# The sums of the attention's probabilities: DMAs that accumulate in SBUF in place of additions on GpSimd

## The chip, the core and the metric

The kernel runs on one core of a Trainium2 chip. The metric is the device time of one execution in microseconds (us). The core has five engines with a queue each: TensorE (PE, matrix products), VectorE (DVE), ScalarE (ACT), GpSimd (POOL) and SyncE (SP), which here issues nearly all DMAs. The engines work on SBUF and meet through semaphores; each serves its queue in order.

## The reference, cut to what matters

One layer of a diffusion backbone over 1024 latent tokens and 128 prompt tokens: a gated feed-forward half-step, a mixer of two attention branches, and a second half-step. The mixer is where the change lies.

```python
# branch A: windowed, 8 heads; a latent token sees 256 cached keys, its own block of 128 and both neighbours, and a sink
p = jax.nn.softmax(jnp.concatenate([s_band, s_ctx, col], axis=-1), axis=-1)
o = einsum(p[..., :lb], vband) + einsum(p[..., lb:lb + lc], vc)
...
# branch B: latent, 8 heads; a latent token sees 256 cached keys and all 1024 latent keys
p = jax.nn.softmax(s, axis=-1)
return jnp.einsum('bkgqs,bskd->bqkgd', p, vf)
```

A softmax needs, for each query, the sum of the exponentials over all its keys. How the kernel adds them up is what the change touches.

## The kernel before, in words

The first feed-forward step and the projections come before the attention, the merge and the second feed-forward step after it; the attention runs from about 1148 to 1830 us. In the attention the keys lie on the partitions and the queries along the free dimension. Heads are worked one after the other: eight windowed ones (to about 1393 us), then eight latent ones.

`attend` (line 1220) works a head in units. A unit is two or three pieces of scores, each of one tile of 128 keys and up to 512 queries, put side by side in a tile of up to 1024 columns. The 1024 queries are cut into two halves of 512. A half has three units in a windowed head and five in a latent head. For each unit:

- TensorE writes the scores to PSUM (`S`, lines 1405 to 1420).
- ScalarE takes the exponential (line 1286). The first unit of a half writes it to a new tile `acc`, the others to a tile `pf`. There are two buffers of each.
- The exponentials are split into a high part `ph` (line 1290 on ScalarE, or line 1288 on VectorE in every second unit) and a low part `pl` (line 1291, a VectorE subtraction of two SBUF operands). Both parts go into the products with the values (lines 1240 and 1241), one unit later.
- In all units of a half but the first, `pf` is added to `acc` (line 1298). In a latent head that is one instruction of 128x1024 for each unit, four a half. In a windowed head a unit needs two, as its pieces cover different queries: 256 and 2x256 columns, which do not overlap, then twice 384 columns, which do. These are four a half too, 128 in the kernel.

When a half is done, `den` (line 1249) folds `acc` (line 1251: its right 512 columns are added to the left on GpSimd), and four steps of the stream later TensorE multiplies it with a column of ones (line 1256), which gives the sums over the partitions; VectorE takes the reciprocal (line 1263), and a DMA puts it into `rec_sp`, for the normalisation of the outputs (line 1456).

The order of the work is that of emission: `attend` is the main stream, and side streams advance with it at set rates (operands and maxima of the next head, the prompt's own attention, gate products and the windowed outputs' product as filling for TensorE). The attention and its side streams are placed 20 instructions ahead of what was emitted before them. Waits between engines follow from which columns of which tile an instruction reads and writes.

Of the kernel before, what the change touches and what calls it, by code (L numbers as in the profile page):

```python
# [20 lines left out]
KD = 8            # feature tiles of the model width  # L21
NL = 1024         # latent tokens
NP = 128          # prompt tokens
T = NL + NP
NB = 3            # token blocks
BW = 384
LB = 256          # latent columns of the last block
NF = 22           # feature tiles of the ffn width
NCTX = 256
NK = NCTX + NL    # keys a latent token reads  # L30
# [6 lines left out]
ADA = ((0, 4), (4, 2), (6, 4), (10, 4), (14, 4))      # first chunk of 512 modulation columns, chunks  # L37
MODS = ((0, 0), (0, 1), (1, 0), (2, 0), (2, 1), (3, 0), (3, 1), (4, 0), (4, 1))   # group and place of each

# cut of the hidden tiles, for both half-step ffns  # L40
SOLO = ((3, 3), (3, 3))   # hidden tiles that the first block runs ahead by
MID = ((2,) * 8, (2,) * 8)
END = ((2, 2, 2), (2, 2, 2))
NA = (6, 6)       # tiles of hidden activations
LAST = ((), (2,))         # blocks whose squares the tensor engine sums tile by tile
NS = 2            # tiles that those sums lag by
TT = ("t0h", "t0l", "t1h", "t1l", "t2h", "t2l")

# steps of side streams per step of the main one
NR = 3            # statistics of the first norm  # L50
NQ = 1.5          # first norm
TR = 1.4          # norm of the second ffn
AR = (2, 0.4)     # modulations, up to the first gate and after it
N2 = (0.5, 1, 2)          # norm of the mixer, by block
FR = (0.3, 1.2, 1.5)      # final norm, by block
CH = 2.6          # latent projections
PREP = (1.3, 1.3, 2.5)    # operands and maxima of the next head: windowed, latent, first latent
PROMPT = 0.5      # prompt's own attention
GRATE = (0.5, 0.7, 0.4, 0.5)   # filling work, by four heads
PR = 0.2          # normalised outputs, windowed  # L60
LR = 0.6          # normalised outputs, latent

# orders and distances
RW = 3            # steps between a block's statistics and their use
DY = 4            # steps before a denominator's product
HM = 2            # one high part in so many is cut off by the vector engine
HP, HQ = 20, 20   # instructions that attention and its side streams come ahead of
GK = 2            # feature tiles of a gate product at a time
G0 = 9            # gate steps before the first head
WN = 5            # step of the merge that loads the first output weights  # L70
# [6 lines left out]
class Build:  # L77
# [45 lines left out]
    def ahead(self, gen, n):  # L123
        """a stream whose instructions come before others emitted up to n earlier"""
        while True:
            if n:
                with self.tc.high_priority(n):
                    try:
                        next(gen)
                    except StopIteration:  # L130
                        return
            else:
                try:
                    next(gen)
                except StopIteration:
                    return
            yield
# [104 lines left out]
    def ada(self, g):  # L242
        """modulations of group g: chunks of 512 columns, each in its own rows of one bank"""
        nc, a = self.nc, self.a
        c0, n = ADA[g]
        ps = self.ps("m")

        def load(k):
            raw = self.ap.tile([P, 2048], F32, name="adaw")[:, :n * 512]
            nc.sync.dma_start(raw, a["ada_w"][k * P:(k + 1) * P, c0 * 512:(c0 + n) * 512])  # L250
            return raw
        raw = load(0)
        for k in range(KD):
            yield
            for cg in range(n):
                nc.tensor.matmul(ps[32 * cg:32 * cg + 32, :], self.cs[:, k, :],
                                 raw[:, cg * 512:(cg + 1) * 512], start=(k == 0), stop=(k == KD - 1))
            if k < KD - 1:
                yield
                raw = load(k + 1)  # L260
        yield
        r = 32 * n
        pt = self.ps("m")
        for q in range(0, 4, 2):
            ev = self.tmp(2 * P)
            nc.vector.tensor_copy(ev[:r, :], ps[:r, q * P:(q + 2) * P])
            for i in range(2):
                nc.tensor.transpose(pt[:, (q + i) * P:(q + i) * P + r], ev[:r, i * P:(i + 1) * P], self.ident[:r, :r])
        yield
        for cg in range(n):  # L270
            j = 4 * (c0 + cg)
            nc.vector.tensor_tensor(
                self.mods[g][:, cg * 4:cg * 4 + 4, :],
                pt.rearrange("p (q r) -> p q r", q=4)[:, :, cg * 32:cg * 32 + 2],
                self.adab[:, j:j + 4][:, :, None].broadcast_to([P, 4, 2]),
                op=ALU.add)
        # scale of norm i = modulation 3i+1, gate = 3i+2
        for i in range(3):
            if MODS[3 * i + 1][0] == g:
                t = self.G[i]  # L280
                nc.vector.tensor_scalar_add(t, self.mod(3 * i + 1), 1.0)
                nc.vector.tensor_mul(t, t, self.gains[:, i, :][:, :, None].broadcast_to([P, KD, 2]))
            if MODS[3 * i + 2][0] == g:
                nc.vector.tensor_scalar_mul(self.gate[i], self.mod(3 * i + 2), 0.5)
        yield

# [33 lines left out]
    def sums(self, ps, sq, start, stop):  # L320
        """sum over the features of one tile, by token on the partitions"""
# [7 lines left out]
    def stat(self, b, k):  # L329
        """sum of squares of a block, one feature tile more"""  # L330
# [78 lines left out]
    # x += gate * psum  # L409
# [51 lines left out]
    def inv(self, b, stats=False):  # L461
        """1 / rms of a block"""
        if stats:
            yield from self.stats(b)
        self.r[b] = yield from self.rstd(self.acc[b], D, RW)

    def norm_pair(self, i):
        """norm of the last two blocks, and sums of their feature halves, for seven products in place of eight;
        the sum of the first halves takes the place of the last block's own"""
# [49 lines left out]
    def gu_pair(self, wgu, j, rest, end=False):  # L519
        """gate and up of the last two blocks in seven products of halves; rest: the first block too"""  # L520
# [75 lines left out]
    def ffn(self, wgu, wd, gate, after, n, begin=None):  # L596
        """the first block runs ahead until the halves of the others are combined; they catch up at the end"""
# [68 lines left out]
    def first(self):  # L666
        """first hidden tiles of the first block, begun with the half of the features that is ready first"""
# [68 lines left out]
    def ada0(self, hf):  # L736
        """shift and scale of the first norm, for half of the features"""
# [72 lines left out]
    def mix(self):  # L810
# [52 lines left out]
        def put(dh, dl, src, w, rows=slice(0, P), shape=None):  # L863
            """two exact parts of src, to DRAM"""
# [20 lines left out]
        def keys(lh, ll, k0, n, prompt):  # L885
            """keys and values of the latent branch from columns of ckv; k0: where they go"""
# [69 lines left out]
        def ctx():  # L956
            """cached keys and values of both branches"""
# [109 lines left out]
    def chain(self, gen, rate):  # L1067
        """like spawn, but one after the other"""
# [11 lines left out]
    def gates(self):  # L1080
        nc = self.nc

        def one(i, b, w):
# [7 lines left out]
            # sigmoid(x) = (1 + tanh(x / 2)) / 2; the half goes with the residual gate  # L1091
# [40 lines left out]
    def rows(self, m, dsts):  # L1132
        # -m of [128, 8 tiles] as rows of the moving operand, in two parts
# [86 lines left out]
    def attend(self, units, S, V, scale, hid):  # L1220
        """units: two parts (key tile, q0, q1) of one width; S(ps, part) writes scores less the maximum."""
# [46 lines left out]
        for n, u in enumerate(units):  # L1268
# [23 lines left out]
            if u[0][0] != 0:  # L1292
                av = acc[hf].rearrange("p (a b) -> p a b", a=2)
                i = 0
                while i < np_:
                    a0 = u[i][1] - 512 * hf
                    m = 2 if i + 1 < np_ and u[i + 1][1] == u[i][1] else 1
                    nc.gpsimd.tensor_add(av[:, :m, a0:a0 + w], av[:, :m, a0:a0 + w], pf[:, i:i + m, :])  # L1298
# [18 lines left out]
    def prompt(self, hid):  # L1317
        """a head over the prompt's own keys"""
# [122 lines left out]
    def normed_o(self, b, br, p):  # L1441
        """outputs of two heads for a block, over their denominators, in two parts"""
# [27 lines left out]
    def fill(self):  # L1470
        """work that the attention's gaps take: gates, then the product of the windowed heads' outputs"""
# [26 lines left out]
    def merge(self):  # L1498
# [15 lines left out]
        def gated(b):  # L1514
            """sum of the gated branches"""
# [74 lines left out]
def _tables():  # L1590
# [19 lines left out]
    # key on partitions; column c stands for query - key block start = c - 256  # L1610
# [5 lines left out]
def _layout(i):  # L1616
# [3 lines left out]
    def kt(w):                    # (K, N) -> [128, K/128, N]  # L1620
        return w.reshape(w.shape[0] // P, P, w.shape[1]).transpose(1, 0, 2)

    def tiles(w):                 # (K, N) -> [N/128, 128, K]
# [10 lines left out]
    def col(v):                   # (n,) -> [128, n/128]  # L1634
# [24 lines left out]
    def small(w):                 # (256, n, 128) -> [128, n * 2 * 128]  # L1659
# [28 lines left out]
```

## Time and profile before

| | us |
|---|---|
| time, median of 3 runs | 2835.97 |
| lowest, highest | 2833.17, 2837.92 |
| span of the profiled execution (its whole time is not listed apart) | 2830.5 |
| PE busy | 2684.0 |
| DVE busy | 1910.4 |
| ACT busy | 971.5 |
| POOL busy | 776.6 |

The profile is of one execution. A span runs from the first to the last instruction; what the device spends around it is the difference to a run's time. Shares of busy time are over the whole span, and the stages differ: the attention has to be read by itself. A row of a group gives the line, engine, operation, tiles written and read, the count, the busy time and mean duration of one, and behind the bar the idle time of the engine just before them with what ended it. Matmuls overlap, so their mean duration is longer than their distance. A DMA counts as busy only for the engines that move data; the row of the issuing queue shows the issue alone.

### The profile page before, as it was taken

What the parts mean: (1) busy time and instruction counts of PE and PEld (TensorE: products, weight loads), DVE (VectorE), ACT (ScalarE), POOL (GpSimd) and SP (SyncE); (2) the same over time, 40 slices, a digit from 0 to 9 for tenths busy, and PEclk for the clock granted to TensorE, in tenths of its full rate; (3) what the DMA queues carried; (4) which work ended last, traced back from release to release, by engine and by line L of the source; (5) the groups of instructions that cost most, each with busy time, mean ns of one, the idle gap of its engine ahead of it and who ended that gap; (6) DMA issues with size and microseconds to landing.
All of it is one profiled execution on the core that took longest, in us unless ns stands there. A gap on an engine that the chain in (4) does not pass through costs nothing.

```text
span 2830.5 us, 38964 instructions
## 1 busy us (share of the span) xinstructions
PE 2684.0 (95%) x15049; PEld 2504.4 (88%) x15049; DVE 1910.4 (67%) x2979; ACT 971.5 (34%) x1492; POOL 776.6 (27%) x523
## 2 busy tenths in 40 slices
PE   7899999999999998999999888899999999999998
PEld 5699999999999897788777766689999999999998
DVE  3765555555687665777788888756685555555777
ACT  4532222222345442344334333324542222222334
POOL 2421111111323011344445444323331111111232
PEclk9899999999999998999999999999999999999999
DMA  7543332111214556223223224485421111111113
GB/s 262 171 139 97 107 112 75 45 45 46 96 52 152 180 178 186 75 80 96 80 73 99 72 77 116 148 277 189 135 89 45 46 45 45 45 46 45 60 60 112
DMA packets 159919, 290.31 MB, mean 103 GB/s; under 512 B 18158, under 2 KB 112866, under 8 KB 156406
## 3 DMA queue, kind: packets, MB, share of 16 engines
q1 hardware_dynamic: 158006, 283.10, 31.9%
q10 hardware_dynamic: 1728, 4.72, 0.4%
q8 instruction: 119, 1.95, 0.3%
q14 instruction: 66, 0.54, 0.1%
HBM read 233.71 MB, written 53.92 MB: 102 GB/s over the span
## 4 chain that ended last, share of the span: by engine, by line
PE 45%; DVE 10%; issue 2%; DMA 2%; ACT 2%; POOL 1%; SPq 0%; DVEq 0%; ACTq 0%; POOLq 0%
PE ps_g L206 7%; PE ps_g L204 7%; PE ps_g L205 7%; PE pp_m L204 4%; PE pp_m L205 4%; PE pp_m L206 4%; DVE pl L1291 3%; PE pp_o L204 1%; PE pp_o L206 1%; PE pp_o L205 1%; PE pp_o L1241 1%; DVE ph L1288 1%; PE pp_m L1212 1%; PE pp_o L1240 1%; PE ps_S L1419 1%
## 5 line engine op out<-in xcount | busy, mean ns | idle before, releaser
L204 PE MATMUL ps_g<-hh,whi 128*128 128x384 f32 x1284 | 435.3, 340 | 10.1 <-ACT hh L175 4.8
L206 PE MATMUL ps_g<-hh,wlo 128*128 128x384 f32 x1284 | 434.9, 339 | 6.0 <-DVE wlo L176 6.0
L205 PE MATMUL ps_g<-hl,whi 128*128 128x384 f32 x1284 | 435.1, 339 | 2.2 <-DVE hl L176 2.2
L543 POOL TENSOR_TENSOR adaw<-adaw 128x512 f32<-128x512 f32 x132 | 182.0, 1379 | 812.7 <-DVE wlo L176 783.6
L176 DVE TENSOR_TENSOR wlo<-raw,whi 128x1024 fp32r<-128x1024 f32 (+1 forms) x203 | 260.5, 1283 | 159.5 <-ACT whi L175 157.6
L1298 POOL TENSOR_TENSOR acc<-acc,pf 128x1024 f32<-128x1024 f32 (+3 forms) x128 | 251.6, 1971 | 406.3 <-ACT pf L1286 213.9
L175 ACT CAST whi<-raw 128x1024 fp32r<-128x1024 f32 (+1 forms) x203 | 209.5, 1033 | 410.8 <-PE ps_g L205 212.9
L175 ACT CAST whi<-adaw 128x1024 fp32r<-128x1024 f32 x132 | 138.9, 1052 | 449.4 <-PE ps_g L205 310.2
L204 PEld LDWEIGHTS ps_g<-hh,whi 128*128 128x128 f32 x1284 | 243.9, 190 | 17.9 <-ACT whi L175 6.2
L206 PEld LDWEIGHTS ps_g<-hh,wlo 128*128 128x128 f32 x1284 | 244.1, 190 | 12.3 <-DVE wlo L176 9.7
L205 PE MATMUL pp_m<-hl,whi 128*128 128x384 f32 x732 | 251.6, 344 | 0.0
L204 PE MATMUL pp_m<-hh,whi 128*128 128x384 f32 x732 | 251.3, 343 | 0.0
L205 PEld LDWEIGHTS ps_g<-hl,whi 128*128 128x128 f32 x1284 | 244.1, 190 | 6.6 <-DVE hl L176 3.1
L206 PE MATMUL pp_m<-hh,wlo 128*128 128x384 f32 x732 | 249.8, 341 | 0.0
L176 DVE TENSOR_TENSOR wlo<-adaw,whi 128x1024 fp32r<-128x1024 f32 x132 | 170.4, 1291 | 105.9 <-ACT whi L175 105.7
L206 PE MATMUL ps_g<-ah,wlo 128*128 128x384 f32 x682 | 229.1, 336 | 2.3 <-DVE wlo L176 2.3
L204 PE MATMUL ps_g<-ah,whi 128*128 128x384 f32 x682 | 230.7, 338 | 0.0
L205 PE MATMUL ps_g<-al,whi 128*128 128x384 f32 x682 | 229.0, 336 | 0.0
L1291 DVE TENSOR_TENSOR pl<-pf,ph 128x1024 fp32r<-128x1024 f32 (+1 forms) x96 | 168.6, 1757 | 4.5 <-ACT ph L1290 2.7
L414 DVE SCALAR_TENSOR_TENSOR y<-ps_g,gate,y 128x384 f32<-128x384 f32 (+2 forms) x271 | 126.8, 501 | 40.4 <-PE ps_g L206 40.0
L204 PEld LDWEIGHTS pp_m<-hh,whi 128*128 128x128 f32 x732 | 140.4, 192 | 8.6 <-issue 2.6
L205 PEld LDWEIGHTS pp_m<-hl,whi 128*128 128x128 f32 x732 | 140.1, 191 | 8.3 <-issue 4.4
(487 smaller groups left out, 6207.9 us busy)
## 6 DMA issues: line engine op xcount, KB each, us to landing
adaw<-gu SPq DMA_DIRECT2D x66, 512.0 KB
raw<-wd SPq DMA_DIRECT2D x52, 512.0 KB
adaw<-ada_w SPq DMA_DIRECT2D x24, 1024.0 KB
raw<-gu SPq DMA_DIRECT2D x46, 512.0 KB
raw<-win SPq DMA_DIRECT2D x27, 512.0 KB
raw<-wout SPq DMA_DIRECT2D x24, 512.0 KB
raw<-wo SPq DMA_DIRECT2D x16, 512.0 KB
gate_sp<-tmp SPq DMA_DIRECT2D x42, 192.0 KB
```

What stands on the lines that cost most here:

```text
L175: self.nc.scalar.copy(hi, src)
L176: (eng or self.nc.vector).tensor_sub(lo, src, hi.bitcast(F32))
L204: nc.tensor.matmul(ps, wh[:, c], mh, start=(start and i == 0), stop=False)
L205: nc.tensor.matmul(ps, wh[:, c], ml, start=False, stop=False)
L206: self.mm = nc.tensor.matmul(ps, wl[:, c], mh, start=False, stop=(stop and i == n - 1))
L414: nc.vector.scalar_tensor_tensor(x[:, d, c0:c1], ps[:, c0:c1], gate[:, d, c:c + 1], x[:, d, c0:c1], op0=ALU.mult, op1=ALU.add)
L543: nc.gpsimd.tensor_tensor(o, x, y, op=op)
L1212: nc.tensor.matmul(ps, q1[0:96, t * P:(t + 1) * P], k1[0:96, c0:c1], start=True, stop=True)
L1240: nc.tensor.matmul(out, V(kt), ph[:, i, :q1 - q0], start=(first[hf] == (n, i)), stop=False)
L1241: nc.tensor.matmul(out, V(kt), pl[:, i, :q1 - q0], start=False, stop=end)
L1291: nc.vector.tensor_sub(pl, pf, ph.bitcast(F32))
L1298: nc.gpsimd.tensor_add(av[:, :m, a0:a0 + w], av[:, :m, a0:a0 + w], pf[:, i:i + m, :])
```

## The change

The sum of `pf` into `acc` is no longer an instruction of GpSimd but a DMA, issued from GpSimd's queue, that reads `pf` in SBUF and adds it to `acc` in SBUF. The loop, the columns, the buffers and their order stay as they were, and so does the fold of line 1251 on GpSimd. All other lines of the diff take out comments, docstrings or blank lines.

```diff
@@ -1295,7 +1295,7 @@
                 while i < np_:
                     a0 = u[i][1] - 512 * hf
                     m = 2 if i + 1 < np_ and u[i + 1][1] == u[i][1] else 1
-                    nc.gpsimd.tensor_add(av[:, :m, a0:a0 + w], av[:, :m, a0:a0 + w], pf[:, i:i + m, :])
+                    nc.gpsimd.dma_start(av[:, :m, a0:a0 + w], pf[:, i:i + m, :], accum_op=ALU.add)
                     i += m
             queue.append((ph, pl))
             if n:
```

## Rows read from the trace of the kernel before

**Rows 1.** The page: busy us of an engine, share of the span, instructions.
```profile
PE 2684.0 (95%) x15049; PEld 2504.4 (88%) x15049; DVE 1910.4 (67%) x2979; ACT 971.5 (34%) x1492; POOL 776.6 (27%) x523
```

**Rows 2.** Stretches: length, busy us (count) of PE PEld DVE ACT POOL, clock, DMA share, GB/s.
```profile
1148.00:1393.00 245.00, 233.65 (x1449) 202.81 (x1448) 186.02 (x345) 96.82 (x159) 105.67 (x80) 0.97 0.29 82
1393.00:1587.00 194.00, 176.34 (x863) 140.65 (x862) 170.18 (x207) 76.63 (x101) 99.86 (x40) 0.99 0.31 84
1587.00:1830.00 243.00, 203.99 (x924) 162.22 (x923) 202.76 (x237) 89.00 (x121) 100.46 (x40) 0.93 0.34 100
```

**Rows 3.** The chain of waits, 1148 to 1830 us: shares by line, a long piece.
```profile
by line: DVE pl L1291 13.4%; PE pp_m L205 6.8%; PE pp_m L204 6.8%; PE pp_m L206 6.4%; PE pp_o L1241 5.3%; DVE ph L1288 5.2%; issue 5.0%; PE pp_m L1212 4.9%; PE pp_o L1240 4.4%; PE ps_S L1419 3.4%; PE ps_S L1420 3.4%; PE ps_S L1418 3.1%; DVE
...
1485.30 3.25 DVE pl L1291
```

**Rows 4.** What TensorE waited for, 1148 to 1830 us: us, times, longest.
```profile
PE pp_o L1241 <- DVE pl L1291: 34.2, 28, 3.6
```

**Rows 5.** Groups of VectorE by shape, 1148 to 1830 us.
```profile
L1291 DVE TENSOR_TENSOR pl<-pf,ph 128x1024 fp32r<-128x1024 f32 x64 | 121.6, 1901 | 1.8 <-ACT ph L1290 0.9
...
L1291 DVE TENSOR_TENSOR pl<-pf,ph 128x768 fp32r<-128x768 f32 x32 | 47.0, 1469 | 2.7 <-ACT ph L1290 1.8
L1291 DVE TENSOR_TENSOR pl<-acc,ph 128x1024 fp32r<-128x1024 f32 x32 | 40.5, 1267 | 19.4 <-ACT ph L1290 19.4
L1288 DVE CAST ph<-pf 128x1024 fp32r<-128x1024 f32 x32 | 35.1, 1095 | 9.8 <-ACT pf L1286 9.8
```

**Rows 6.** Timeline of VectorE and GpSimd in a latent head: start, us, instruction.
```profile
1479.06 0.67 DVE L1288 CAST ph<-pf 128x1024 fp32r<-128x1024 f32 x1
...
1479.83 1.23 DVE L1291 TENSOR_TENSOR pl<-pf,ph 128x1024 fp32r<-128x1024 f32 x1
...
1483.56 3.90 POOL L1298 TENSOR_TENSOR acc<-acc,pf 128x1024 f32<-128x1024 f32 x1 [0.25 <-ACT pf L1286]
...
1485.30 3.24 DVE L1291 TENSOR_TENSOR pl<-pf,ph 128x1024 fp32r<-128x1024 f32 x1
```

**Rows 7.** Groups of GpSimd by shape, 1100 to 1900 us.
```profile
L1298 POOL TENSOR_TENSOR acc<-acc,pf 128x1024 f32<-128x1024 f32 x64 | 171.9, 2686 | 234.8 <-ACT pf L1286 140.2 <-DVE pl L1291 90.7 <-ACT hh L175 2.9
```

**Rows 8.** Timeline of a latent head: exponentials that begin a half, a fold, its product.
```profile
1490.30 1.02 ACT L1286 ACTIVATE acc<-ps_S 128x1024 f32<-128x1024 f32 x1 [4.45 <-PE ps_S L1420]
...
1509.36 1.27 POOL L1251 TENSOR_TENSOR acc<-acc 128x512 f32<-128x512 f32 x1
...
1522.47 0.43 PE L1256 MATMUL pp_m<-acc,ones 128*32 128x128 f32 x8
...
1537.90 1.03 ACT L1286 ACTIVATE acc<-ps_S 128x1024 f32<-128x1024 f32 x1 [3.52 <-PE ps_S L1420]
```

**Rows 9.** Timeline of the first half and of the last: sums, fold, product.
```profile
1154.46 5.74 POOL L1298 TENSOR_TENSOR acc<-acc,pf 128x256 f32<-128x256 f32 x4 [50.35 <-DVE pl L1291]
1160.27 2.13 POOL L1251 TENSOR_TENSOR acc<-acc 128x512 f32<-128x512 f32 x1
...
1163.53 0.66 PE L1256 MATMUL pp_m<-acc,ones 128*32 128x128 f32 x8
...
1814.79 2.71 POOL L1298 TENSOR_TENSOR acc<-acc,pf 128x1024 f32<-128x1024 f32 x1 [1.90 <-ACT pf L1286]
1817.58 1.33 POOL L1251 TENSOR_TENSOR acc<-acc 128x512 f32<-128x512 f32 x1
1820.07 0.38 PE L1256 MATMUL pp_m<-acc,ones 128*32 128x128 f32 x2 [2.87 <-DVE tmpx L1489]
```

**Rows 10.** A small load: size, chain piece, issue; and the first stretch (columns: rows 2).
```profile
kp<-kAP SPq DMA_DIRECT2D x6, 32.0 KB
...
1306.91 1.97 DMA kp<-kAP
...
1306.91 0.59 SPq L1329 DMA_DIRECT2D kp<-kAP  x1
...
0.00:30.00 30.00, 12.86 (x98) 5.61 (x98) 5.93 (x15) 10.35 (x18) 8.77 (x12) 1.00 0.95 339
```

## The prediction, made before the result was known

> **What bounds the kernel now.** I read the page first. Over the whole span TensorE is busy 95%, VectorE 67% and GpSimd 27% [rows 1], so over the whole kernel TensorE sets the time. The change lies in the attention alone, so the stretches come second: from 1148 to 1830 us TensorE is busy 233.65 + 176.34 + 203.99 = 614 of 682 us, and idle 68 us; outside it the change touches nothing. In the windowed heads (1148 to 1393 us) TensorE is busy 95% and VectorE 76%; in the latent heads (1393 to 1830 us) TensorE falls to 87% and VectorE rises to 85% [rows 2]. So the windowed heads are bound by TensorE, and the latent heads by TensorE and VectorE in turn. The chain of waits of that stretch, third, says where: 13.4% of it is the subtraction that makes pl, and 5.2% the copy that makes ph, both VectorE; its longest single pieces are subtractions of over 3 us [rows 3]. The waits agree: what TensorE waits for most is pl, 34.2 us at the product with the low parts [rows 4].
>
> Why a subtraction takes 3 us is read from groups and timeline together. Of one shape, 128x1024, it takes 1267 ns on average when its input is acc, but 1901 ns when it is pf; with pf there is a GpSimd sum of the same pf at the same time [rows 5]. In the timeline the subtraction that starts at 1479.83 us, before a sum, takes 1.23 us; the one at 1485.30 us, while GpSimd works on a sum begun at 1483.56 us, takes 3.24 us. It ends 1.08 us after that sum, about one undisturbed subtraction later [rows 6]. I read this as VectorE being held until the sum is over.
>
> **The change, part by part.** The diff has one line that emits instructions; the rest are comments and blank lines and cost nothing.
>
> *What it removes.* 128 sums on GpSimd: 64 of 128x1024 at 2686 ns, 171.9 us of GpSimd, and 64 narrower ones [rows 7]. GpSimd itself bounds nothing, so their own time is worth nothing; their worth is what they do to VectorE. With 1.23 us as the undisturbed subtraction [rows 6], and 0.92 us for one of 768 columns (the same by columns), pl gains 64 x (1.90 - 1.23) + 32 x (1.47 - 0.92) + 32 x (1.27 - 1.23) = 43 + 18 + 1 = 62 us of 121.6 + 47.0 + 40.5 = 209 us, 30% [rows 5]. The ph copy of pf takes 1095 ns on average against 0.68 us undisturbed, 38% [rows 5, 6]. On the chain pl holds 13.4% of 682 = 91 us and ph 35 us [rows 3]: 91 x 0.30 + 35 x 0.38 (upper, as ph has other forms) = 27 + 13 = 40 us. Not all of it comes back: TensorE has work of its own for 90% of the stretch, and the gate products that now fill its gaps must still be done. Ends: 0 (TensorE is next at once) and 40 us. I take half, 20 us, nearer to neither, since TensorE's whole idle time there is 68 us, and a late pl causes about half of that [rows 2, 4].
>
> *What it adds.* 128 DMAs issued from GpSimd's queue, each of which reads pf and acc and writes acc in SBUF. The trace has no accumulating DMA and none from GpSimd, so the time L from issue until the sum may be read is bounded by the nearest rows. A 32 KB load lands 1.97 us after its issue began [rows 10]: the fixed part. The 16 engines moved 339 GB/s in the first 30 us, at a share of 0.95 [rows 10]; 512 KB then take 1.55 us for each pass. One pass gives L = 3.5 us, two passes (both operands read, the write alongside) 5.1 us, three in a row 6.6 us. Making the descriptors on GpSimd in place of SP may add some 0.5 us, and SP's own transfers, a share of 0.31 to 0.34 now [rows 2], can lengthen some. I take 5.1 us, the middle: that rate was held back by HBM on one side, and this copy stays in SBUF. For the narrow ones of 192 to 256 KB two passes give 3.1 to 3.5 us.
>
> The Trainium skill (DMA: Bandwidth & Descriptors, "Anatomy of one DMA") puts a DMA from GpSimd at some 2.0 us and its bytes at 436 GB/s. With both operands counted that would be an estimate of 4.4 us, and by it the stalls below would be near nothing; no run here shows it yet.
>
> *The wait it adds.* Four sums of a half of a latent head go into the same acc, so each DMA must wait on GpSimd until the one before it has landed, and behind it in GpSimd's queue stand the next sum, the fold of acc's two halves (1.27 us undisturbed [rows 8]) and then the next half's sums. One half therefore takes at least 4 L + 1.3 us: 21.7 us at L = 5.1. From 1393 to 1587 us eight halves take 194 us, 24.3 us each; later 243 / 8 = 30.4 us [rows 2]. So the chain of DMAs is hidden up to L = (24.3 - 1.3) / 4 = 5.75 us in the faster heads and 7.3 us in the others. In the windowed heads the first two sums touch other columns and can run side by side, so a half needs about 3 x 3.3 + 1.3 = 11.2 us of 245 / 16 = 15.3 us: hidden.
>
> Two others wait. ScalarE's exponential for the pf after next writes into the buffer that the DMA reads; it comes about 9.7 us later (a head of 47.6 us [rows 8] has ten units), so up to that it is hidden. TensorE's product of acc with ones waits for the fold: usually 12 us lie between (1510.6 to 1522.5 us [rows 8]), but only 1.1 us in the first half (fold over at 1162.40, product at 1163.53) and 1.2 us in the last (1818.91 to 1820.07) [rows 9]. There the later sum shows. In the last half the last DMA begins at 1814.79 and would let the fold end at 1814.79 + 5.1 + 1.3 = 1821.2, 1.1 us late; in the first half the chain begins at 1154.46 and ends near 1154.46 + 3.3 x 3 + 1.3 = 1165.7, 2.1 us late. With some 2 us for transfers that meet a head's loads I take 5 us of stalls (0 at L = 3.5).
>
> *Sum.* -20 + 5 = -15 us: a span of 2830.5 - 15 = 2815.5 us, and with the 5.5 us by which the median of 2835.97 us stands above the profiled span, 2821 us. Nothing else moves: SP's order is kept, and the only other GpSimd work of the stretch is the fold.
>
> **The rivals.**
>
> *A. The chain of DMAs becomes the bound: slower.* From L = 5.75 us each half of the faster heads takes 4 L + 1.3 us whatever VectorE gains, because GpSimd serves the sums in order and acc is one buffer for the half. With three passes and the 0.5 us for descriptors, L = 7.1: 29.7 us a half, 5.4 x 8 = 43 us more, and some 10 us from the products of acc that now come late: 2836 + 53 = 2889 us. At L = 8 it is 33.3 us a half: 9.0 x 8 + 2.9 x 8 = 95 us, 2931 us. TensorE would then also stand idle more, and the stretch in which it is idle most already has the lowest granted clock: 0.93 from 1587 us on, where it is idle 39 of 243 us, against 0.99 before [rows 2]. For it: the sums may add three passes and SP's transfers, and the margin is 0.65 us. Against it: SBUF on both sides.
>
> *B. The relief is given back: no change.* The subtraction gets short, but the latent heads go no faster, since TensorE's products, ScalarE's exponentials and the DMAs at L of 5.5 to 6 us together keep the old pace: 2831 to 2841 us. For it: TensorE is busy 90% of the stretch. Against it: 34.2 us of waiting for pl alone [rows 4].
>
> *C. VectorE and GpSimd still get into each other's way.* The ph copy of every second unit starts when its exponential ends, and so would the issue of the DMA. If GpSimd, writing descriptors, holds that copy as its sums do now, by up to 0.6 us (the nearest row, SP's issue of a DMA, takes 0.59 us [rows 10]), 64 copies cost 38 us of VectorE, half of it on the path: -15 + 19 = +4 us, 2840 us. For it: the copy is lengthened now, 1095 ns against 0.68 us [rows 5, 6]. Against it: that is already in the time before, and a descriptor is far less data than a sum. The Trainium skill (SBUF — State Buffer, "Who interferes with whom") states the same exclusion the other way round: fast VectorE copies lock GpSimd out while it writes descriptors. By it L would grow by up to the copy's 0.67 us in every second unit, 4 L + 1.3 to 23.0 us, still under 24.3 us; the trace has no such DMA to show it.
>
> **How the numbers follow.** L decides: under some 5.4 us the forecast holds, to 6 us the two effects cancel, above it A. My chances: forecast 0.48, A 0.34, B 0.12, C 0.06. The forecast's own range is 2796 (all of the 40 us) to 2830 us. The range over all cases reaches up into A: 2796 to 2905 us (A at L = 7.4 us), which leaves out less than 2 in 10, nearly all of it above. A measurement of this kernel tells 0.2%, 5.7 us, from no change: faster 0.48, same 0.13 (most of B and part of C), slower 0.39.
>
> **What would show it.** Right: pl from pf near 1.2 us on average in place of 1.90, VectorE's busy time in the attention down by 60 us or more, its share of the chain down, and TensorE busy over 90% in the latent heads; folds on GpSimd that start within about 5 us of the last exponential of a half; no row in which ScalarE's exponential or TensorE's product with ones waits for a DMA into acc, but in the first and last half. Wrong: exponentials that wait for DMAs into acc, evenly spaced at about L; GpSimd's queue waiting for DMAs all through a half; halves of the latent heads longer than 25 us; a granted clock under 0.9 in the stretch. If pl gets short and the halves still keep 24 us, B holds and TensorE is the bound. A sum of 2931 us or more would mean that L was mis-sized by more than every row here allows.

## The result, and the profile after

| | before | after |
|---|---|---|
| time, median of 4 runs (us) | 2834.57 | 2860.12 |
| lowest, highest | 2822.87, 2837.92 | 2851.8, 2865.83 |
| ratio, 95% interval | | 1.0102 [1.0072, 1.0131] |
| span of the profiled execution | 2830.5 | 2864.1 |

The change makes the kernel 1.0% slower. The forecast was 2821 us, faster; the time lies inside the range of 2796 to 2905 us, between the forecast and rival A.

The page of after shows what was meant to happen, against [rows 1]: VectorE is 113.5 us less busy and GpSimd 142.5 us less. The part on queues shows the new load, GpSimd's queue q0 with 46 MB, and the part on the chain of waits gives these DMAs 8% of the whole span.

```profile
PE 2695.0 (94%) x15049; PEld 2520.5 (88%) x15049; DVE 1796.9 (63%) x2979; ACT 970.0 (34%) x1492; POOL 634.1 (22%) x523
...
q0 software_dynamic: 20480, 46.15, 9.3%
...
DMA acc<-pf 8%; PE ps_g L206 7%; PE ps_g L205 7%; PE ps_g L204 7%; PE pp_m L204 3%; PE pp_m L205 3%; PE pp_m L206 3%; PE pp_o L204 1%; PE pp_o L206 1%; PE pp_o L205 1%; POOL acc L1251 1%; PE pp_o L1240 1%; PE pp_o L1241 1%; POOL acc L1298 1%; PE pp_m L1212 1%
```

The groups of VectorE by shape, 1148 to 1860 us, answer to [rows 5]. The subtraction from pf falls from 1901 to 1218 ns, that of 768 columns from 1469 to 967, the copy to ph from 1095 to 690. VectorE is not held any more. These groups and the subtraction from `acc` make up 74 of the 113.5 us; the rest lies in smaller VectorE instructions that got shorter too (two kinds of updates of `mrow`, 15 each, fall by 12 us together).

```profile
L1291 DVE TENSOR_TENSOR pl<-pf,ph 128x1024 fp32r<-128x1024 f32 x64 | 78.0, 1218 | 24.5 <-ACT ph L1290 21.8 <-PE ps_S L1420 1.7
...
L1291 DVE TENSOR_TENSOR pl<-pf,ph 128x768 fp32r<-128x768 f32 x32 | 30.9, 967 | 4.7 <-ACT ph L1290 4.0
...
L1288 DVE CAST ph<-pf 128x1024 fp32r<-128x1024 f32 x32 | 22.1, 690 | 26.7 <-ACT pf L1286 25.8 <-PE pp_o L1240 0.9
```

The waits of all engines, 1140 to 1900 us (us in total, times, longest), show what took its place. GpSimd waits 306.8 + 113.3 us for its own DMAs. ScalarE's exponential waits 94.7 us until a DMA has read its buffer `pf`, and TensorE's product of `acc` with ones waits 40.4 us for the fold. TensorE's wait for pl at line 1241, 34.2 us before [rows 4], is 3.4 us now.

```profile
POOL acc L1298 <- DMA acc<-pf: 306.8, 69, 7.5
POOL acc L1251 <- DMA acc<-pf: 113.3, 27, 7.2
ACT pf L1286 <- DMA acc<-pf: 94.7, 28, 8.1
...
PE pp_m L1256 <- POOL acc L1251: 40.4, 9, 7.4
```

The chain of waits, 1148 to 1860 us, against [rows 3]: VectorE's subtraction held 13.4% of it, and now the DMAs into `acc` hold a third, in pieces of 3 to 8 us.

```profile
by line: DMA acc<-pf 33.6%; issue 15.9%; PE pp_m L205 4.4%; PE pp_m L204 4.4%; PE pp_m L206 4.2%; POOL acc L1251 3.5%; PE pp_o L1240 3.4%; PE pp_o L1241 3.2%; POOL acc L1298 2.7%; PE pp_m L1212 2.2%; PE ps_S L1420 1.8%; PE ps_S L1410 1.8%;
...
1424.65 7.12 DMA acc<-pf
...
1467.55 4.56 DMA acc<-pf
1472.76 4.80 DMA acc<-pf
```

The timeline of GpSimd over one half of a latent head shows the links: four issues 5.21, 5.44, 5.21 and 4.59 us apart, the last up to the fold, each but the first behind a wait for the DMA before it.

```profile
1467.55 0.88 POOL L1298 DMA_DIRECT2D acc<-pf  x1
1472.76 0.86 POOL L1298 DMA_DIRECT2D acc<-pf  x1 [4.33 <-DMA acc<-pf]
1478.20 0.86 POOL L1298 DMA_DIRECT2D acc<-pf  x1 [4.58 <-DMA acc<-pf]
1483.41 0.87 POOL L1298 DMA_DIRECT2D acc<-pf  x1 [4.35 <-DMA acc<-pf]
1488.00 1.98 POOL L1251 TENSOR_TENSOR acc<-acc 128x512 f32<-128x512 f32 x1 [3.72 <-DMA acc<-pf]
```

Over all 64 of the latent heads the distance from one issue to the next instruction of GpSimd, which is what a link means below, runs from 1.99 to 8.83 us, with a median of 5.96 and a mean of 6.07 us. In a half the fold now starts 12.4 us after the last exponential on average, in place of 3.4 us before. By stretches, against [rows 2], TensorE's granted clock is lower where it waits, 0.93 and 0.91 (columns as there; windowed, then latent heads):

```profile
1149.00:1411.00 262.00, 236.25 (x1448) 207.44 (x1447) 161.11 (x343) 96.42 (x159) 83.34 (x80) 0.93 0.59 124
1411.00:1854.00 443.00, 381.45 (x1760) 308.09 (x1759) 280.64 (x441) 164.22 (x220) 83.19 (x80) 0.91 0.73 167
```

### The profile page after: what moved, and what is told of

The parts are those of the page before. It is cut to its first block, busy times and chain, and to the rows that moved or that the text cites. A ratio compares the mean times of both kernels' runs of the same rounds, so it can differ in the third digit from the quotient of the medians.

```text
span 2864.1 us, 39014 instructions
## 1 busy us (share of the span) xinstructions
PE 2695.0 (94%) x15049; PEld 2520.5 (88%) x15049; DVE 1796.9 (63%) x2979; ACT 970.0 (34%) x1492; POOL 634.1 (22%) x523
## 4 chain that ended last, share of the span: by engine, by line
PE 41%; DMA 10%; issue 5%; POOL 2%; DVE 2%; ACT 1%; SPq 1%; POOLq 0%; DVEq 0%; ACTq 0%
DMA acc<-pf 8%; PE ps_g L206 7%; PE ps_g L205 7%; PE ps_g L204 7%; PE pp_m L204 3%; PE pp_m L205 3%; PE pp_m L206 3%; PE pp_o L204 1%; PE pp_o L206 1%; PE pp_o L205 1%; POOL acc L1251 1%; PE pp_o L1240 1%; PE pp_o L1241 1%; POOL acc L1298 1%; PE pp_m L1212 1%
## 5 line engine op out<-in xcount | busy, mean ns | idle before, releaser
L1298 POOL DMA_DIRECT2D acc<-pf x128 | 123.8, 999 | 454.7 <-DMA acc<-pf 306.8
L1286 ACT ACTIVATE pf<-ps_S 128x1024 f32<-128x1024 f32 (+1 forms) x96 | 91.6, 954 | 238.0 <-DMA acc<-pf 94.7
```

Source lines behind the costliest of these rows:

```text
L1286: nc.scalar.activation(pf, ps, AF.Exp, scale=scale)
L1298: nc.gpsimd.dma_start(av[:, :m, a0:a0 + w], pf[:, i:i + m, :], accum_op=ALU.add)
```

## The experiments

Fifteen kernels ran, each against the kernel before on the same chip. Their differences to the change, which was set against the kernel before in a set of runs of its own, are differences of two ratios, of 2830 us. "Windowed" is the stretch of the profiled execution from the first exponential into `acc` to that of the first latent head, "latent" from there to the last product of `acc` with ones. These are from one execution each (that of the change took 5.7 us more than the median). Where the windowed heads of two kernels are the same, as in 14 and before or in 13 and the change, the stretch differs by 4 to 5 us, so differences of that size are not read. Kernels 6, 7, 8, 11 and 12 also have one buffer of `oraw`, the raw outputs, in place of two; no kernel has that alone.

| kernel | ratio to before, 95% interval | windowed | latent |
|---|---|---|---|
| before | 1 | 243.8 | 430.2 |
| the change | 1.0102 [1.0072, 1.0131] | 261.1 | 443.8 |
| 1 no sums | 0.9691 [0.9675, 0.9708] | 229.3 | 351.9 |
| 2 copies without chain | 0.9694 [0.9680, 0.9709] | 227.5 | 354.8 |
| 3 half the columns | 0.9878 [0.9864, 0.9893] | 242.4 | 393.6 |
| 4 DMAs in windowed heads only | 1.0056 [1.0037, 1.0076] | 253.9 | 425.7 |
| 5 windowed: 2 links, not 3 | 1.0042 [1.0027, 1.0057] | 239.9 | 439.0 |
| 6 latent: two accumulators | 0.9965 [0.9951, 0.9978] | 258.4 | 401.2 |
| 7 both 5 and 6 | 0.9924 [0.9901, 0.9948] | 240.8 | 403.9 |
| 8 third buffer of pf | 1.0015 [0.9999, 1.0032] | 250.3 | 422.1 |
| 9 product of acc 8 steps late | 1.0074 [1.0057, 1.0091] | 261.2 | 428.0 |
| 10 last unit on GpSimd | 0.9933 [0.9917, 0.9948] | 232.8 | 415.5 |
| 11 as 10, third buffer of pf | 0.9872 [0.9857, 0.9887] | 232.9 | 396.9 |
| 12 as 11, product 6 steps late | 0.9855 [0.9840, 0.9869] | 237.1 | 386.7 |
| 13 change, keys loaded once | 0.9966 [0.9951, 0.9981] | 255.7 | 406.1 |
| 14 before, keys loaded once | 1.0009 [0.9997, 1.0021] | 239.4 | 435.6 |
| 15 two units of a half on GpSimd | 1.0008 [0.9996, 1.0021] | 239.6 | 427.3 |

The theory: the DMAs into one `acc` form a serial chain that sets the pace, and that eats more than VectorE's relief gives. Its rivals: that the relief is worth little, or that the added traffic is what costs.

### 1 to 4: the relief, the traffic, the chain, the stage

**1, no sums:** the DMA is left out.

```diff
-                    nc.gpsimd.dma_start(av[:, :m, a0:a0 + w], pf[:, i:i + m, :], accum_op=ALU.add)
+                    pass
```

> The sums over key tiles are left out altogether: neither GpSimd nor a DMA adds pf to acc. Chain theory (the change frees VectorE, and its DMAs, one after another into one acc, then bind): 20 to 40 us faster than before, ratio 0.986 to 0.993, pl from pf near 1.22 us, no products of acc that wait. Rival 'no relief' (TensorE bounds the stretch, a shorter pl is worth nothing): within 6 us of before.

2740.36 us against 2830.43: 3.1% faster, some 88 us. The 20 to 40 us expected were far too few. So much was to be had from taking the sums off GpSimd, and the DMAs then cost 4.1%, 116 us. The stretches (windowed, latent) show how: TensorE is idle for 1.2 us in all, at a clock of 0.99 and 1.00.

```profile
1148.00:1377.00 229.00, 228.21 (x1446) 198.78 (x1446) 162.33 (x346) 97.51 (x161) 21.44 (x16) 0.99 0.31 90
1377.00:1729.00 352.00, 351.61 (x1753) 287.48 (x1751) 280.88 (x439) 164.13 (x218) 22.50 (x16) 1.00 0.39 110
```

**2, the same columns without a chain:** each DMA copies `pf` plainly to a place of its own in HBM.

```diff
-                    nc.gpsimd.dma_start(av[:, :m, a0:a0 + w], pf[:, i:i + m, :], accum_op=ALU.add)
+                    nc.gpsimd.dma_start(self.junk[self.nj, :, :m * w].rearrange("p (i c) -> p i c", i=m), pf[:, i:i + m, :])
+                    self.nj += 1
...
```

> Each of the 128 DMAs copies the same columns of pf from GpSimd's queue, but to a place of its own in HBM and without adding: the sums are left out, the issues, the buffers that pf waits for and the bytes moved once remain, nothing waits for an earlier DMA. Chain theory: nearly as fast as without the sums, within 6 us of it, 15 to 40 us faster than before. Rival 'traffic' (46 MB more in the attention delay SP's loads and stores): 10 us or more slower than without the sums, near or above the time before.

2741.79 us, as fast as without any sums. 128 DMAs of the same size from the same queue, and a DMA share of 0.46 and 0.64, cost nothing that can be measured when none waits for another; ScalarE waits 0.4 us in all for `pf`, against 94.7 us with the change. This is less traffic than the change's, whose share is 0.59 and 0.73: a plain copy reads `pf` alone and writes to HBM. So the experiment prices the issues, the buffers and these bytes, and not the reading and writing of `acc`. A copy of 512 KB lands after 3.9 us (last column), an accumulating one of the change after 5.4.

```profile
junk<-pf POOLq DMA_DIRECT2D x64, 512.0 KB, 3.9
```

```profile
acc<-pf POOLq DMA_DIRECT2D x64, 512.0 KB, 5.4
```

**3, half the columns:** the DMA adds only the left half of each piece.

```diff
+                    hw = w // 2
+                    nc.gpsimd.dma_start(av[:, :m, a0:a0 + hw], pf[:, i:i + m, :hw], accum_op=ALU.add)
```

> Each accumulating DMA takes only the left half of its columns (the right half of the sums is left out); the chain of DMAs into acc stays, each link moves half the bytes. Chain theory: a link of the latent heads falls from 5.2 to 6.1 us to about 3.5 to 4.2 us, a half needs 4 x 3.9 + 1.3 = 17 us and is hidden: faster than before by 10 to 35 us. Rival 'latency' (it is the fixed part of a link, its wait and issue, that costs): still slower than before, by 5 to 20 us.

0.9878: as many links, each shorter, and about half of the 4.1% gone. 256 KB land after 4.3 us, so half the bytes shorten a landing by only a fifth, and the mean link falls from 6.07 to 5.23 us, where 3.5 to 4.2 were expected. A latent half still takes 22.4 us from its first issue to its fold's end, as much as a half of kernel 1 takes in all (352 / 16 = 22.0).

**4, the windowed heads alone** take DMAs; the latent ones keep GpSimd's addition (`if br == 1`).

> DMAs add in the windowed heads only; in the latent heads GpSimd adds as before. In the profile of the change the windowed stage is 17 us and the latent stage 16 us longer than before. Chain theory: 10 to 17 us slower than before, as the links of a windowed half, two at a time, take 13 to 14 us of about 15 us and the folds come late for TensorE. The step of my prediction (the windowed heads' DMAs are hidden, 11 of 15 us): within 6 us of before.

1.0056: slower by itself, 10 us longer in the windowed stretch. These heads are not hidden either. The change's timeline of GpSimd, here over one half of a windowed head, shows the chain: the first two DMAs side by side hold the next up for 7.6 us, then links of 3.4 and 3.1 us, and the fold, 15.3 us from the first issue to the fold's end.

```profile
1317.37 2.11 POOL L1298 DMA_DIRECT2D acc<-pf  x2
1324.94 0.92 POOL L1298 DMA_DIRECT2D acc<-pf  x1 [5.46 <-DMA acc<-pf]
1328.33 0.87 POOL L1298 DMA_DIRECT2D acc<-pf  x1 [2.47 <-DMA acc<-pf]
1331.39 1.25 POOL L1251 TENSOR_TENSOR acc<-acc 128x512 f32<-128x512 f32 x1 [2.19 <-DMA acc<-pf]
```

The last exponential of that half had ended long before, at 1317.54 us. TensorE comes to the product of `acc` and stands idle for 3.66 us:

```profile
1332.70 0.65 PE L1256 MATMUL pp_m<-acc,ones 128*32 128x128 f32 x8 [3.66 <-POOL acc L1251]
```

The granted clock is 0.66 on average over the 4 us in which the wait ends, and 0.50, which is 1.2 of 2.4 GHz, in the next 4 us, with TensorE busy all the time; then it is back (columns as in [rows 2]):

```profile
1326.00:1330.00 4.00, 3.04 (x19) 2.45 (x18) 3.29 (x10) 2.59 (x6) 0.87 (x1) 1.00 0.65 142
1330.00:1334.00 4.00, 1.30 (x14) 0.76 (x14) 0.36 (x2) 0.00 (x0) 2.61 (x3) 0.66 0.26 43
1334.00:1338.00 4.00, 4.00 (x16) 3.16 (x15) 1.09 (x2) 0.26 (x1) 0.71 (x1) 0.50 0.77 119
1338.00:1342.00 4.00, 4.00 (x25) 3.92 (x25) 1.52 (x2) 0.81 (x1) 0.92 (x1) 0.99 0.72 155
```

So a wait of 3.66 us is followed by at least 4 us at half speed, which lose about 2 us more.

From the first issue of a half to its fold's end the change takes 15.2 us on average in the windowed heads (13.2 to 19.1 in full chains) and 25.7 us in the latent ones. 16 of them are 243 of 262 us and 411 of 443 us: GpSimd's chain fills 93% of both stretches. In the kernel before, the same measure, from a half's first sum to its fold's end, is about 8 and 19 us, 53 and 71%. Of the 655 us of the chains GpSimd waits 420 for its own DMAs. That the chain sets the pace is read from this; experiments 5, 6 and 10 test it by shortening it.

### 5 to 9: shorter chains, more room

**5, two links for three** in the windowed heads: the second piece of a half's last unit goes into the other, unused lane of `acc`, so that it need not wait for the first.

```diff
+                    lane = int(m == 1 and i == 1)
-                    nc.gpsimd.dma_start(av[:, :m, a0:a0 + w], pf[:, i:i + m, :], accum_op=ALU.add)
+                    nc.gpsimd.dma_start(av[:, lane:lane + m, a0:a0 + w], pf[:, i:i + m, :], accum_op=ALU.add)
```

> As the change, but in the windowed heads' last unit of a half the second piece goes to acc's other 512 columns (the fold adds both anyway), so its DMA no longer overlaps the first piece's and need not wait for it: two links of a chain in place of three, same bytes, same number of DMAs. Chain theory: the windowed stage loses some 20 to 35 us of its 262, the latent stage nothing: 5 us faster to 8 us slower than before. Rival 'latency of the fold' (it is the last link and the fold, not the number of links, that come late): within 6 us of the change, 20 to 30 us slower than before.

1.0042, and the windowed stretch falls from 261.1 to 239.9 us with the same bytes and the same number of DMAs. The mean chain of a half is 13.0 us in place of 15.2. The latent stretch keeps its length within what such stretches differ by (439.0).

**6, two accumulators** in the latent heads: units 0, 2, 4 go into `acc` and units 1, 3 into a second tile `odd`, which GpSimd adds at the fold. The room comes from one buffer of `oraw`.

```diff
...
+            elif br == 1 and u[0][0] == 2:
+                pf = odd[hf] = self.Pp.tile([P, 1024], F32, name="odd", bufs=1)
...
-                av = acc[hf].rearrange("p (a b) -> p a b", a=2)
+                av = (odd if br == 1 and u[0][0] % 4 == 2 else acc)[hf].rearrange("p (a b) -> p a b", a=2)
...
```

> As the change, but a latent half has two accumulators: the exponential of its second unit goes straight into a second tile, the third and fifth unit are added to the first, the fourth to the second; GpSimd adds the two before the fold. Links one after another fall from four to two; DMAs of a half from four to three. To make room the tile of raw outputs has one buffer. Chain theory: the latent stage comes near that without sums, 45 to 70 us shorter than with the change; windowed stage as with the change: 20 to 45 us faster than before. Rival 'links' (a link of 5 to 8 us holds pf's two buffers whatever it waits for): within 10 us of before.

0.9965, 10 us faster than before and 39 us faster than the change; the latent stretch falls from 443.8 to 401.2 us. That is short of the 20 to 45 us expected, and within what the rival allowed against before, though the rival has no reason for the 42.6 us that the stretch loses. A quarter of the bytes of these heads is gone too, as `odd` needs no first sum; experiment 2 makes it unlikely that this is the gain, without showing it.

**7, both.**

> The two edits together, other lanes in the windowed heads and two accumulators in the latent heads. Chain theory: 50 to 80 us faster than before, near the time without sums (90 us faster), as 16 sums on GpSimd and the late folds remain. Rival 'links': no more than 20 us faster.

0.9924, 21 us below before, which is less than was expected. The windowed stretch is that of 5 and the latent one that of 6, so the two edits add up, and no more than that. From first issue to fold's end a half now takes 13.0 and 19.4 us, less than the 14.3 and 22.0 us that a half of kernel 1 takes in all, and still the kernel is 66 us slower than kernel 1: a short chain is not enough. A part that shows is the new tile's single buffer, for which ScalarE waits until GpSimd has added it, and the folds, for which TensorE still waits; how the 66 us divide is open.

```profile
ACT odd L1290 <- POOL acc L1252: 39.4, 11, 5.4
...
PE pp_m L1258 <- POOL acc L1253: 23.8, 6, 6.2
```

**8, a third buffer of `pf`** (`bufs=3`, and one of `oraw`): ScalarE can run a unit further ahead of the chain.

> As the change, with three buffers of pf in place of two (room: one buffer of raw outputs). ScalarE waits 94.7 us for pf's DMAs in the change. Chain theory: a buffer more shifts that wait but no link gets shorter, and a latent half still takes 4 links and the fold: 0 to 10 us faster than the change, still slower than before by 15 us or more. Rival 'buffer' (the wait for pf's buffer is the cost): 40 us or more faster than the change, faster than before.

1.0015, 25 us better than the change, and ScalarE's wait for a DMA falls from 94.7 to 29.8 us. TensorE's wait for the fold rises from 40.4 to 64.2 us: the chain is nearly as long as it was (14.8 and 25.3 us a half for 15.2 and 25.7) and shows at its other end. The gain is more than the 0 to 10 us expected of a chain that alone sets the pace, so the buffer's waits were a cost of their own.

```profile
PE pp_m L1256 <- POOL acc L1251: 64.2, 19, 8.5
...
ACT pf L1286 <- DMA acc<-pf: 29.8, 9, 5.8
```

**9, the product of `acc` 8 steps after the fold** (`DY = 8`).

> As the change, but the product of acc with ones comes eight steps of the stream after the fold is emitted, in place of four. With the change TensorE waits 40.4 us there in nine places. Chain theory: those waits go, the links stay (a latent half still takes 4 x 6.1 + 1.3 = 25.7 us): 5 to 20 us faster than the change, still slower than before by 5 us or more. Rival 'late fold' (the cost of the change is the fold that comes late for TensorE): the whole cost goes, 40 us or more faster than the change.

1.0074; its interval and that of the change overlap, so a gain is not shown. TensorE's wait for the fold is halved, to 20.5 us, and the windowed stretch stays at 261.2 us all the same: ScalarE waits longer for its buffer there (15.4 us for 9.7), and TensorE then for ph. The latent stretch of the profiled execution is 16 us shorter (428.0). Room at one end of a chain does not make it shorter: a half's chain is 15.1 and 25.4 us.

### 10 to 12: a version faster than both

**10, the last unit of each half on GpSimd**, the others by DMA, so that no landing lies between the last exponential and the fold.

```diff
+                    if last[hf][0] == n:
+                        nc.gpsimd.tensor_add(av[:, :m, a0:a0 + w], av[:, :m, a0:a0 + w], pf[:, i:i + m, :])
+                    else:
                         nc.gpsimd.dma_start(av[:, :m, a0:a0 + w], pf[:, i:i + m, :], accum_op=ALU.add)
```

> As the change, but the sum of the last unit of each half is made by GpSimd as before, the others by DMAs (64 + 32 of 128 fewer DMAs: three links in a latent half, one in a windowed half, and none right before the fold). Chain theory: a latent half needs 3 x 5.7 + 2.4 + 1.3 = 21 us of GpSimd's time, a windowed half about 5 + 2.6 + 1.3 = 9 us; VectorE is still held by one sum of a half in place of four: latent stage 385 to 405 us against 444 with the change and 430 before, 25 to 50 us faster than before. Rival 'links' (a link holds pf's two buffers): within 15 us of before.

0.9933: a windowed half has one pair of unchained DMAs left, and its stretch (232.8 us) is near that without sums. The latent stretch, 415.5 us, is longer than the 385 to 405 expected, and the gain on before, 19 us, is short of 25 to 50: a latent half still takes 23.2 us from first issue to fold's end, and ScalarE waits 49.0 us for `pf`. (80 of 128 DMAs are left, 48 fewer; the expectation miscounts them.)

**11** adds the third buffer of `pf`, **12** also `DY = 6`.

> The run before this one with three buffers of pf and one of raw outputs. Chain theory: with three links a half has room, so the third buffer takes the rest of ScalarE's waits for DMAs: 10 to 25 us faster than with two buffers, 40 to 70 us faster than before. Rival 'traffic and links' : no gain from the buffer.

> The same with the product of acc with ones six steps after the fold is emitted, in place of four. Chain theory: takes what is left of TensorE's waits for folds: 0 to 10 us faster than e11, 45 to 80 us faster than before. Rival: no change against e11, as the fold is in time there.

0.9872 and 0.9855. Kernel 12 computes all sums, takes 2786.82 us against 2827.45 and has the lowest ratio of those that do: 1.5% faster than before, 2.4% than the change. The intervals of 11 and 12 overlap, so that the last edit helps is not shown. Against before the two gain 36 and 41 us, each some 4 us less than the least expected. On its chain of waits the DMAs hold 5.8% in place of 33.6%, behind TensorE's products:

```profile
by line: PE pp_m L204 8.7%; PE pp_m L206 8.4%; PE pp_m L205 8.4%; PE pp_o L1241 7.6%; PE pp_o L1240 7.5%; DMA acc<-pf 5.8%; PE pp_m L1212 5.3%; PE ps_S L1423 4.6%; PE ps_S L1422 4.5%; PE ps_S L1421 4.5%; issue 3.5%; DVE ph L1288 2.6%; PE ps
```

It is still 46 us above experiment 1; what those are is open.

### 13 to 15: what lengthens a link

**13 and 14, keys and values loaded for the first latent head only**, in the change and in the kernel before.

```diff
+        if h == 0:
+            self.kvB = self.qk("k1", NK), self.qk("k2", NK), self.qk("v", NK)
+        k1, k2, vt = self.kvB
...
```

> The change, with the loads of keys and values left out for all latent heads but the first (they use the first head's): some 1.6 MB of SP's transfers for a head less, of about 2.4. If SP's loads lengthen the links: DMAs into acc land in 4.6 to 4.9 us in the median of the 512 KB ones (5.4 with the change), a latent half takes 4 x 5.4 + 1.3 = 23 us, the latent stage falls from 444 to 380 to 415 us: 25 us or more faster than the change. If the accumulating DMA sets its time alone: 5.2 us or more to landing, within 10 us of the change.

> The kernel before with the same loads left out: the control. Both theories: within 6 us of before, as no engine waits long for those loads there.

The loads themselves stand behind the same condition. Without them the change gains 1.4%, 38 us; the kernel before gains nothing (1.0009). 512 KB land after 5.0 us for 5.4, between the two expectations. The mean distance of two links falls from 6.07 to 5.82 us, 64 x 0.25 = 16 us; ScalarE's wait for `pf` falls from 94.7 to 41.9 us, while TensorE's for the fold rises from 40.4 to 47.4. So the chain suffers from other transfers, and the kernel before does not. How the other 22 us divide between the clock (0.95 for 0.91) and waits is open.

Two landings of the change show the same, one with few transfers beside it and one with SP's loads of the next head's keys and queries, issued from 1716.5 to 1719.6 us (columns as in [rows 2], the DMA share and GB/s last): 4.56 us at a share of 0.63, 8.19 us at 0.97.

```profile
1467.55:1472.11 4.56, 4.29 (x27) 3.48 (x28) 3.38 (x6) 1.15 (x2) 0.88 (x2) 1.00 0.63 121
1718.96:1727.15 8.19, 7.11 (x34) 5.98 (x34) 4.97 (x5) 4.55 (x6) 1.28 (x1) 1.00 0.97 224
```

**15, two links left in a latent half**: its last two units go to GpSimd (`or br == 1 and u[0][0] > 4` beside the condition of 10), with `DY = 6` and two buffers of `pf`.

> As the change, but GpSimd makes the sums of the last two units of a latent half and of the last unit of a windowed half, DMAs the others (two links in a latent half); the product of acc with ones comes six steps after the fold is emitted; two buffers of pf as with the change. Chain theory: hardly any wait for a DMA into acc is left (ScalarE under 15 us), but VectorE is held by two sums of a half: 25 to 45 us faster than before, no faster than e12 by more than 5 us. Rival 'links': 10 us faster than before at most.

1.0008: a miss, 25 to 45 us were expected. Fewer links are not better when GpSimd takes the rest: kernel 10, with one more link a half and the same two buffers, had 0.9933. ScalarE's wait for `pf` is 42.2 us where less than 15 was expected. GpSimd's additions wait 69.9 us for the DMAs ahead of them in the same tile and queue, and VectorE is held again: pl from pf takes 1455 ns, and TensorE waits 18.0 us for it. The groups of the latent stretch:

```profile
L1299 POOL TENSOR_TENSOR acc<-acc,pf 128x1024 f32<-128x1024 f32 x32 | 84.7, 2647 | 73.2 <-DMA acc<-pf 69.9 <-ACT pf L1286 2.3
...
L1291 DVE TENSOR_TENSOR pl<-pf,ph 128x1024 fp32r<-128x1024 f32 x64 | 93.0, 1455 | 1.9 <-ACT ph L1290 1.0
```

## Why the prediction was wrong

**Which engine was held, and why: right.** The durations that [rows 5, 6] gave for the freed VectorE, 1.23 and 0.92 us, are those of after, 1.22 and 0.97. The list was too short: pl and ph gave 74 us of VectorE's 113.5, and the rest, in small instructions, was not counted.

**What that is worth: the term was mis-sized.** I put 20 us, halfway between 0 (TensorE "is next at once") and 40, because TensorE was busy for 614 of 682 us. Experiment 1 gives 88 us. TensorE's 614 busy us were not a floor. Without sums its idle time there falls from 68 to 1.2 us and its busy time to 580 us (in a stretch that ends some 8 us earlier), at a clock of 0.99 to 1.00 in place of 0.93 to 0.99 [rows 2]. So some 26 us of busy time went with no work left out on TensorE; the mean clock of [rows 2], 0.96, accounts for about 21 of them (614 x 0.035, an estimate). Removing waits also removed the slow time behind them. Taken alone, this error would have made the forecast too slow.

**The price of one undisturbed DMA: nearly right.** L was put at 5.1 us; a latent link with few transfers beside it takes about 5.2 us, and 512 KB land after 5.4 us in the median. The estimate from the Trainium skill (DMA: Bandwidth & Descriptors, "Anatomy of one DMA") was 4.4 us with both operands counted; the trace has 5.4.

**The step that failed: "hidden".** The forecast said that a half's chain of 4 L + 1.3 = 21.7 us is covered by 24.3 us, and the windowed one of 11.2 by 15.3, with 5 us of stalls. It fails on both sides: L as the chain pays it is 6.07 us on average, above the 5.75 us that I had worked out as the limit, a latent half's chain takes 25.7 us and a windowed one 15.2. Measured, the DMAs cost 116 us over what no sums cost, in both stages (32 and 92 us in the profiled executions). Four things were missing:

- The cover itself was to shrink. The pace to stay under is that of the relieved kernel: 352 / 16 = 22.0 us a latent half and 229 / 16 = 14.3 a windowed one. At 22.0 us the limit for L is (22.0 - 1.3) / 4 = 5.2 us, not 5.75.
- "Some 2 us" for transfers that meet a head's loads was a mean link of 6.07 us for 5.1, 16 x 4 x 0.97 = 62 us of chain. Experiment 13 confirms the cause in part: 16 us of it by distance, 38 us by time.
- The windowed chain was put at 3 x 3.3 + 1.3 = 11.2 us and takes 15.2, above the 14.3 us of the relieved pace. The links take 6.2, 4.2 and 4.0 us on average where 3.3 stood for each. The first is mis-sized most: two DMAs "side by side" were counted as one, and the second of them has landed only 4.7 to 7.9 us after the first issue.
- A chain as long as its half has waits at both ends: `pf` has two buffers and comes free at the pace of the links (ScalarE 94.7 us), and the product of `acc` comes before the fold (TensorE 40.4 us). I held the exponential's distance of 9.7 us (9.5 by the figures beside it) against one L, although the DMA is itself issued late by the links before it, and looked for late folds in the first and the last half alone. Experiments 5, 6, 8 and 10 each shorten the chain or relax an end, and give back 17, 39, 25 and 48 us.

**The rivals.** A is what happened, at a lower price: it asked for L from 5.75 us, the mean is 6.07, and GpSimd's queue waits for DMAs all through the halves, as it said. Its 2889 us were worked out at L = 7.1 and without the gain of 88 us that stands against it. With 6.07 its own sum gives 25.6 us a half, 1.3 x 8 + 10 = 20 us more and 2856 us; that this is near 2860 is in part luck, as it leaves the windowed heads, which cost 32 of the 124 us, out. The other signs came too: latent halves of 27.7 us (443.8 / 16) in place of under 25, and a granted clock of 0.89 from 1609 to 1860 us, just under the 0.9 named. B fails: the relief is large and is lost again, not absent. C fails: ph takes 690 ns, so issuing a DMA does not hold VectorE. Nor did the traffic of experiment 2 cost anything by itself, a rival that I formed after the result; the change's own, with `acc` read and written, was not tried without a chain.

## What to carry to other kernels

Sums that follow one another into one tile are cheap by DMA only if something else covers the landing of each. Count the links between the last input and the first reader, and set their sum against the pace that the kernel will have after the gain, not the pace that it has. An engine that reads 95% busy may be so because it ran slowly behind waits; leave the work out once to see what its removal is worth, before pricing its replacement. Two accumulators or the last term on an engine shortened the chain here; one more buffer eased the wait at its end. None of them reached the time without sums.

## What the runs showed of the chip that was not expected

In the median an accumulating DMA from SBUF to SBUF of 512 KB lands after 5.4 us, of 256 KB after 4.3 (experiment 3) to 4.4, of 192 KB after 3.3 and of 128 KB after 2.8 us; a plain copy of 512 KB to HBM, from the same queue, after 3.9 us.

GpSimd is busy 0.85 to 0.93 us with most issues that stand alone in the trace of the change. Of these 97, 15 took 1.21 to 1.31 us, and all 15 overlap a copy of VectorE to ph, as here (the first row is GpSimd's, the second VectorE's); of the 74 that overlap no such copy none took over 0.93. Eight more overlap one, seven of them for under 0.5 us, and take 0.86 to 1.03 us.

```profile
1451.34 1.30 POOL L1298 DMA_DIRECT2D acc<-pf  x1 [5.09 <-DMA acc<-pf]
```

```profile
1451.86 0.69 DVE L1288 CAST ph<-pf 128x1024 fp32r<-128x1024 f32 x1 [3.66 <-ACT pf L1286]
```

The Trainium skill (SBUF — State Buffer, "Who interferes with whom") says that a fast VectorE copy locks GpSimd out while it writes descriptors. The trace agrees, at some 0.4 us for an issue; that is far less than what the waits for landings cost.
